# A one-core mLSTM layer with feed-forward: queries split behind the scores, token tiles transposed a turn later, the last output weights, the last chunk's output and the gate's start put in another order

## The chip, the cores and the metric

One core of a Trainium2 chip runs the whole kernel. The metric is the time of one execution in device microseconds. The kernel before was run three times and once more with the profiler.

## The reference

One layer over 2048 tokens of width 1024, in float32:

```python
xn = rmsnorm(h, norm_mix)
u = xn @ w_in                          # q, k (4 heads x 128), v, o (4 x 256), gates
h_fwd = mlstm_scan(q, k, v, g[0], g[1])
h_bwd = flip(mlstm_scan(flip(q), flip(k), flip(v), flip(g[2]), flip(g[3])))
h = rms(h_fwd + h_bwd, per head) * head_norm * sigmoid(o)
h1 = x + h @ w_out
h1 = h1 + square(relu(rmsnorm(h1) @ w1)) @ w2
gate = sigmoid(rmsnorm(h1) @ ple_gate_w + ple_gate_b)
out = rmsnorm(h1 + gate * (p @ ple_w))
...
def step(carry, xs):                   # mlstm_scan, one chunk of 128 tokens
    s = einsum('bhtd,bhsd->bhts', q_, k_) * d
    num = einsum('bhts,bhsv->bhtv', s, v_) + inter * einsum('bhtd,bhvd->bhtv', q_, C)
    den = sum(s) + inter * (q_ . n)
    h = num / max(abs(den), exp(-m_t))
    C = decay * C + einsum('bhsv,bhsd->bhvd', w * v_, k_)
```

## The kernel before, in words

Each float32 operand of a product is split into a high part (a copy rounded to fp32r on ScalarE, ACT) and a low part (a subtraction on VectorE, DVE, or GpSimd, POOL), and `mm3` (L185) makes a product of three matmuls from them. SyncE (SP) and POOL issue the loads and stores, in order on each queue. Instructions are written in a program order; the framework's scheduler then orders each engine's instructions by its own estimate of when they are ready, and each engine works through its list in that order. Most instructions have the line of a helper (L100), so they are told apart by the names of tiles.

Stages: the input projection; the backward scan, woven into the rest of the projection; then the forward scan over 16 chunks of 128 tokens, which also combines both directions and multiplies by `w_out`; the feed-forward part (up jobs, down jobs), written as seven products of half-size blocks each; and last, token tile by token tile, the gate, the second projection and the final norm.

**The forward scan (L683 to L821, L1372 to L1420).** In turn c the program works on several chunks at once. `ORDER` (L1373) is the list of steps of a turn; `step` (L1375) gives what each stands for:

- `n0`, `n1`: numerators of chunk c for both directions (`nums`): for each head a bank pn of six matmuls, then a copy nt on ACT. `s`: state update of chunk c (four banks pu, Cn on DVE, Chi on ACT), `sl` its low part Clo.
- `S`, `e`, `w`: scores pS of chunk c+1, the exponentials mb of its decay matrix (ACT, then a mask on POOL, L736), and their product (mb on DVE, pTh, pTl). `q`: `q_split`, the query operands, qsh on ACT and qsl on POOL (L748, L167). `k`: weighted keys wk. `v`: value operands vh, vl.
- `T`, `o0`, `o1`: of chunk c-1 the transposes pth, the gated hThi and hTlo, and the two halves of the output product pso with xt on DVE.
- `m`, `me`: norm of chunk c: rd, nt scaled on ACT and DVE, squares jk, then `rstd` (rsa, rsy, rst) and jk scaled by rsy.
- `d1`, `d2`, `d`, `p`: loads for chunks c+1 (vst, kt, cb) , c (og, xt) and c+2 (kq, mb, ib), and for c+2 ib times the queries on POOL (L726).

From turn `XC` = 7 on, three steps (`Tokens0.steps`, L1009) also prepare a finished token tile of the feed-forward part: `xl` loads it, `xn` normalises it (xs), `xt` transposes it (pt, zt) and stores it (x_d). All three stand in the same turn of `ORDER_X` (L1414); with them tile c-7 is made in turn c.

`TR` (L1390) mixes the end of the projection with chunk 0 and loads (`a0` to `a7`) and splits (`c0` to `c7`) the eight row blocks of `w_out`. `TAIL` (L1421) is the last chunk, with the first operands of the feed-forward part: `Z` loads, `U` block sums, `X` splits, `P` the first up job's left operands, `T15`, `y0`, `y1` the transposes and output of chunk 15.

Large tiles take one of 39 buffers of tag H (`Ht`), `raw`, `og`, `xt` and `zt` one of 7 of tag O (`Ot`). PSUM has four banks for pn, pu, pso and the product banks pa, pb, pg (`ps_mm`), three for transposes, pl and pc (`ps_tr`), one for scores and for the gate's token transposes (`ps_s`).

**The gate's start (L1468 to L1503).** The loads and splits of the gate weights `wgt` and of `wpl` (ple_w) and the first token tiles are hung into the last down jobs by `late`. Then, per token tile, `half` makes a half of the gate product pg from xTh, xTl and `wgt`, then pl from the embeddings and `wpl`, and the sum; `tr0` and `tr1` transpose the next tile in two halves, each into the single bank of `ps_s`.

Of the kernel before, what the change touches and what calls it, by code (L numbers as in the profile page):

```python
# [35 lines left out]
def hybrid_mlstm_kernel(  # L36
# [20 lines left out]
    x, p, out = x[0], p[0, 0], out[0]  # L57
# [7 lines left out]
    def ps_mm(name):  # L65
        return psm.tile([P, 512], F32, tag="mm", bufs=4, name=name)
# [614 lines left out]
    wo = [rows_w(w_out, k * P) for k in range(KD)]  # L681
# [500 lines left out]
    wgt = [rows_w(gate_w, k * P) for k in range(KD)]  # L1182
    wpl = [rows_w(ple_w, k * P) for k in range(2)]
# [32 lines left out]
    class Tok:  # L1216
# [21 lines left out]

        tr0, tr1 = (lambda self: self.tr(0)), (lambda self: self.tr(1))

        def half(self, n):

            if n == 0:
                self.ss = small("ssf")
            sl = slice(n * 512, (n + 1) * 512)
            pg = ps_mm("pg")
            tk = slice((self.t % 4) * P, (self.t % 4 + 1) * P)
            for k in range(KD):
                mm3(pg, self.hi[:, k], self.lo[:, k], wgt[k].hi[:, sl], wgt[k].lo[:, sl], k == 0, k == KD - 1)
# [39 lines left out]
    o, q = jobs[0, "o"], jobs[0, "q"]  # L1289
# [50 lines left out]
    for nm, pr in (("k", pa[0][0]), ("q", pa[0][1])):  # L1340
        e = pr.early()
# [7 lines left out]
    u1, u0 = jobs[0, "v"]  # L1349
# [20 lines left out]
    assert len(slots) == len(steps) - 8  # L1370

    ch = [Chunk(c) for c in range(NC)]  # L1372
    ORDER = "n0 d1 s e T S n1 d2 k w q sl m v d o0 o1 me p".split()  # L1373

    def step(c, nm):  # L1375

# [29 lines left out]
    def row_load(nm, src):  # L1406
        rowc[nm] = Ht(f"row_{nm}", [P, D])
        SP.dma_start(rowc[nm], src.partition_broadcast(P))


    XC = 7
    tp = {c: x0.steps(c - XC) for c in range(XC, XC + 8)}
    tp[XC][0] = lambda f=tp[XC][0]: (row_load("mlp", norm_mlp[0]), f())
    ORDER_X = "n0 d1 s e T S n1 d2 k w xl q sl m v d xn o0 o1 xt me p".split()  # L1414
    for c in range(1, NC - 1):
        for nm in ORDER_X if c in tp else ORDER:
            if nm in ("xl", "xn", "xt"):
                tp[c][("xl", "xn", "xt").index(nm)]()
            else:
                step(c, nm)()  # L1420
    TAIL = "d2 W n1 Z1 Z3 T n0 Z2 Z4 o0 m me P1 X1 T15 P2 o1 U3 U1 y0 X2 U2 X3 y1".split()  # L1421
    l = ch[NC - 1]
    u0 = up[0][0]
    extra = {"T15": l.transposes, "y0": lambda: l.out(0), "y1": lambda: l.out(1), "W": u0.left.dma,
             "P1": lambda: [f() for f in u0.prep[:3]], "P2": lambda: [f() for f in u0.prep[3:]],
             "X1": lambda: x0.split("B11"), "X2": lambda: x0.split("B21"), "X3": lambda: x0.split("T2")}
    extra |= {f"Z{i}": lambda nm=nm: x0.zload(nm) for i, nm in ((1, "B11"), (2, "B21"), (3, "B12"), (4, "B22"))}
    extra |= {f"U{i}": lambda i=i: x0.sums(f"T{i}") for i in (1, 2, 3)}
    for nm in TAIL:
        extra[nm]() if nm in extra else step(NC - 1, nm)()  # L1430
# [22 lines left out]
    n = ENTER[-1] + NQ  # L1453
# [14 lines left out]
    pp = [Early_p(t) for t in (0, 4, 8, 12)]  # L1468
    toks = [Tok(t, pp[t // 4]) for t in range(NC)]
    for g in range(4):  # L1470
# [55 lines left out]
```

## Time and profile before

| | us |
|---|---|
| three runs | 2489.95, 2493.55, 2499.76 (median 2493.55) |
| profiled execution | 2496.48 |
| its span, first to last instruction | 2494.8 |
| TensorE matmuls busy in it | 2415.3 |
| VectorE, ScalarE, GpSimd busy | 1525.7, 1134.5, 610.9 |
| TensorE granted clock, mean | 0.99 |

A stretch is read by four views: busy time by stretch (how long, how busy, at which granted clock), waits (who stood still for whom), the timeline of an engine (each instruction with the idle time before it and what ended it), and the durations of all instructions on a tile. `x4` counts instructions merged into a row. PE is TensorE; its matmuls overlap, so a row of 0.39 us can have its successor 0.23 us later.

### The profile page before, as it was taken

What the parts mean: (1) busy time and instruction counts of PE and PEld (TensorE: products, weight loads), DVE (VectorE), ACT (ScalarE), POOL (GpSimd) and SP (SyncE); (2) the same over time, 40 slices, a digit from 0 to 9 for tenths busy, and PEclk for the clock granted to TensorE, in tenths of its full rate; (3) what the DMA queues carried; (4) which work ended last, traced back from release to release, by engine and by line L of the source; (5) the groups of instructions that cost most, each with busy time, mean ns of one, the idle gap of its engine ahead of it and who ended that gap; (6) DMA issues with size and microseconds to landing.
All of it is one profiled execution on the core that took longest, in us unless ns stands there. A gap on an engine that the chain in (4) does not pass through costs nothing.

```text
span 2494.8 us, 31616 instructions
## 1 busy us (share of the span) xinstructions
PE 2415.3 (97%) x11413; PEld 1987.1 (80%) x11413; DVE 1525.7 (61%) x2533; ACT 1134.5 (45%) x2134; POOL 610.9 (24%) x609
## 2 busy tenths in 40 slices
PE   7999999998899999999999999999999999999998
PEld 6988898787778887788878888787887888777776
DVE  5152336456787888656775445766676667655665
ACT  5031324336667885443353333444443444445554
POOL 1040022124433334344733333111111111110000
PEclk9999999999999999999999999999999999999999
DMA  7177337867566765455763331467686776882211
GB/s 250 48 207 238 91 101 243 271 216 276 201 210 212 254 234 190 144 169 169 257 203 125 114 112 59 160 146 178 142 185 166 176 173 153 184 219 84 85 54 49
DMA packets 270134, 420.72 MB, mean 169 GB/s; under 512 B 46441, under 2 KB 181993, under 8 KB 269977
## 3 DMA queue, kind: packets, MB, share of 16 engines
q1 hardware_dynamic: 211416, 299.03, 36.7%
q0 software_dynamic: 58272, 119.15, 20.4%
q8 instruction: 89, 1.46, 0.2%
q14 instruction: 69, 0.56, 0.1%
q10 hardware_dynamic: 288, 0.52, 0.1%
HBM read 253.43 MB, written 165.01 MB: 168 GB/s over the span
## 4 chain that ended last, share of the span: by engine, by line
PE 52%; DVE 4%; DMA 3%; ACT 2%; issue 1%; SPq 0%; POOL 0%; ACTq 0%; DVEq 0%
PE pa L100 26%; PE pb L100 13%; PE pc L100 6%; PE pg L100 5%; DMA hst<-hid_d 1%; PE pl L100 1%; DMA wst<-in_mlp_w 1%; DVE op L100 1%; PE pt L100 1%; DVE h L100 1%; DMA z<-tz_d 1%; ACT L100 1%; DVE xs L100 1%; PE pso L100 1%; DVE rst L100 1%
## 5 line engine op out<-in xcount | busy, mean ns | idle before, releaser
L100 PE MATMUL pa<-op 128*128 128x512 f32 x3072 | 753.2, 394 | 7.6 <-ACT e L100 4.1
L100 PEld LDWEIGHTS pa<-op 128*128 128x128 f32 x3072 | 575.4, 188 | 147.6 <-ACT e L100 7.8
L100 PE MATMUL pb<-op 128*128 128x512 f32 x1536 | 384.3, 394 | 1.2 <-DVE op L100 0.8
L100 PEld LDWEIGHTS pb<-op 128*128 128x128 f32 x1536 | 288.1, 188 | 70.0 <-ACT e L100 1.2
L100 PE MATMUL psf<-xT,whi 128*128 128x512 f32 x1024 | 320.8, 394 | 0.0
L100 DVE TENSOR_TENSOR op<-sa,op 128x768 fp32r<-128x768 f32 (+2 forms) x160 | 167.6, 1053 | 137.9 <-ACT op L100 106.1
L1162 POOL DMA_DIRECT2D h_d<-o x96 | 93.1, 977 | 567.8 <-DVE o L100 507.3
L100 PEld LDWEIGHTS psf<-xT,whi 128*128 128x128 f32 x1024 | 191.3, 188 | 43.7
L100 ACT COPY e<-pa 128x512 f32<-128x512 f32 x160 | 93.7, 586 | 261.6 <-PE pa L100 260.9
L100 ACT CAST op<-sa 128x768 fp32r<-128x768 f32 (+2 forms) x160 | 139.6, 879 | 146.7 <-PE pb L100 66.6
L100 PE MATMUL psf<-xT,wlo 128*128 128x512 f32 x512 | 201.8, 394 | 0.0
L100 PE MATMUL pc<-op 128*128 128x512 f32 x768 | 191.6, 394 | 0.2 <-DVE op L100 0.2
L100 PEld LDWEIGHTS pc<-op 128*128 128x128 f32 x768 | 144.1, 188 | 34.1 <-DVE op L100 0.6
L100 PE MATMUL psv<-whi,xT 128*128 128x272 f32 (+2 forms) x720 | 160.9, 317 | 0.6 <-DVE xT L98 0.6
L100 PEld LDWEIGHTS psv<-whi,xT 128*128 128x128 f32 x720 | 118.6, 188 | 9.8 <-DVE xT L98 0.8
L100 DVE TENSOR_TENSOR op<-wst,op 128x512 fp32r<-128x512 f32 x96 | 108.6, 1134 | 28.7 <-ACT op L100 16.0
L884 POOL TENSOR_TENSOR sa<-wst 128x512 f32<-128x512 f32 x32 | 60.4, 1887 | 263.9 <-PE pb L100 167.6
L100 ACT CAST op<-wst 128x512 fp32r<-128x512 f32 x96 | 79.3, 834 | 93.8 <-DVE op L100 59.3
L100 DVE TENSOR_TENSOR wlo<-wst,whi 128x1024 fp32r<-128x1024 f32 (+2 forms) x64 | 77.1, 1214 | 60.4 <-ACT whi L100 49.4
L100 PE MATMUL psv<-wlo,xT 128*128 128x272 f32 (+2 forms) x360 | 114.0, 317 | 0.0
L100 PEld LDWEIGHTS psf<-xT,wlo 128*128 128x128 f32 x512 | 96.1, 188 | 22.4
L100 PE MATMUL pg<-whi,xTl 128*128 128x512 f32 x256 | 102.5, 400 | 0.0
(228 smaller groups left out, 4318.6 us busy)
## 6 DMA issues: line engine op xcount, KB each, us to landing
wst<-in_mlp_w SPq DMA_DIRECT2D x96, 512.0 KB
h_d<-o POOLq DMA_DIRECT2D x96, 512.0 KB, 12.8
hid_d<-e SPq DMA_DIRECT2D x128, 256.0 KB
hst<-hid_d SPq DMA_DIRECT2D x64, 384.0 KB
wst<-in_mlstm_w_in SPq DMA_DIRECT2D x44, 512.0 KB
vst<-v_d SPq DMA_DIRECT2D x31, 512.0 KB
raw<-in_x SPq DMA_DIRECT2D x16, 512.0 KB
kq<-kq_d SPq DMA_DIRECT2D x16, 512.0 KB
```

Of the source, the lines that this page charges most:

```text
L100: r = f(*a, **kw)
L884: eng.tensor_tensor(s[:, 0], r1[:, :, P:], r2[:, :, P:], op=add_)
L1162: G.dma_start(rows(h1_d, 2 * q + i), o[i], accum_op=add_)
```

## The change

- `q` moves in `ORDER` from behind `w` to right behind `S`, in `ORDER_X` too.
- `XC` is 6, so a tile is loaded and normalised in turns 6 to 13; its transposition `xt` is now made a turn later, behind `n1`, in turns 7 to 14.
- The splits `c6` and `c7` of the last two row blocks of `w_out` move from `TR` into turn 1, with a list of its own (`ORDER_1`, in which `q` keeps its old place).
- The output of chunk 15 (`y0`, `y1`) moves out of `TAIL` behind the first of the seven products of the first up job.
- At the gate's start the first tile's two gate products are made before the splits of ple_w and the first pl, and both transpositions of the second tile stand ahead of these; ple_w is loaded one down job later.

```diff
-        def half(self, n):
+        def gate(self, n):
+            sl = slice(n * 512, (n + 1) * 512)
+            self.pg = pg = ps_mm("pg")
+            for k in range(KD):
+                mm3(pg, self.hi[:, k], self.lo[:, k], wgt[k].hi[:, sl], wgt[k].lo[:, sl], k == 0, k == KD - 1)
+
+        def half(self, n, gate=True):
             if n == 0:
                 self.ss = small("ssf")
-            sl = slice(n * 512, (n + 1) * 512)
-            pg = ps_mm("pg")
+            if gate:
+                self.gate(n)
+            sl, pg = slice(n * 512, (n + 1) * 512), self.pg
             tk = slice((self.t % 4) * P, (self.t % 4 + 1) * P)
-            for k in range(KD):
-                mm3(pg, ...)
...
-    ORDER = "n0 d1 s e T S n1 d2 k w q sl m v d o0 o1 me p".split()
+    ORDER = "n0 d1 s e T S q n1 d2 k w sl m v d o0 o1 me p".split()
...
-        "n1 v b2 q m d c4 a6 me b3 c5 p c6 a7 c7").split()
+        "n1 v b2 q m d c4 a6 me b3 c5 p a7").split()
...
-    XC = 7
+    XC = 6
     tp = {c: x0.steps(c - XC) for c in range(XC, XC + 8)}
-    ORDER_X = "n0 d1 s e T S n1 d2 k w xl q sl m v d xn o0 o1 xt me p".split()
+    ORDER_1 = "n0 d1 s e T c6 S n1 d2 k w c7 q sl m v d o0 o1 me p".split()
+    ORDER_X = "n0 d1 s e T S q n1 xt d2 k xl w sl m v d xn o0 o1 me p".split()
     for c in range(1, NC - 1):
-        for nm in ORDER_X if c in tp else ORDER:
-            if nm in ("xl", "xn", "xt"):
-                tp[c][("xl", "xn", "xt").index(nm)]()
+        for nm in ORDER_X if c in tp or c - 1 in tp else ORDER if c > 1 else ORDER_1:
+            if nm == "xt":
+                tp.get(c - 1, [lambda: None] * 3)[2]()
+            elif nm in ("xl", "xn"):
+                tp.get(c, [lambda: None] * 3)[("xl", "xn").index(nm)]()
+            elif nm in ("c6", "c7"):
+                wo[int(nm[1])].prep()
             else:
                 step(c, nm)()
-    TAIL = "d2 W n1 Z1 Z3 T n0 Z2 Z4 o0 m me P1 X1 T15 P2 o1 U3 U1 y0 X2 U2 X3 y1".split()
+    TAIL = "d2 W n1 Z1 Z3 T n0 Z2 Z4 o0 m me P1 X1 o1 P2 T15 U3 U1 X2 U2 X3".split()
...
+    u0.post[0][:0] = [lambda: l.out(0), lambda: l.out(1)]
...
-            46: [wgt[6].prep, wgt[7].prep, wpl[0].dma, wpl[1].dma, toks[0].tr0, pp[0].split],
-            47: [wpl[0].prep, wpl[1].prep, toks[0].tr1, lambda: row_load("nf", norm_final)]}
+            46: [wgt[6].prep, wgt[7].prep, toks[0].tr0, pp[0].split],
+            47: [wpl[0].dma, wpl[1].dma, toks[0].tr1, lambda: row_load("nf", norm_final)]}
...
-        toks[t].half(0)
+        if t == 0:
+            toks[t].gate(0)
+            pg0 = toks[t].pg
+            nx.tr1()
+            toks[t].gate(1)
+            pg1 = toks[t].pg
+            wpl[0].prep()
+            wpl[1].prep()
+            toks[t].pg = pg0
+        toks[t].half(0, t > 0)
...
-        if nx:
+        if nx and t > 0:
             nx.tr1()
...
-        toks[t].half(1)
+        if t == 0:
+            toks[t].pg = pg1
+        toks[t].half(1, t > 0)
```

How the instructions stand on ACT in turn 1, from the second w_out cast (whi) in the turn on. Before:

```order
L100 CAST whi<-wst 128x1024
L100 ACTIVATE mb<-mb,gcol 128x128 x6
L100 CAST whi<-wst 128x1024
L100 ACTIVATE mb<-mb,gcol 128x128 x2
L100 CAST whi<-wst 128x1024
L100 COPY nt<-pn 128x257 x4
L100 CAST Chi<-Cn 128x1032
L100 CAST hThi<-og 128x512 x2
```

and with the change:

```order
L100 CAST whi<-wst 128x1024
L100 ACTIVATE mb<-mb,gcol 128x128 x3
L100 COPY nt<-pn 128x257 x4
L100 ACTIVATE mb<-mb,gcol 128x128 x5
L100 CAST Chi<-Cn 128x1032
L100 CAST hThi<-og 128x512 x2
L100 CAST whi<-wst 128x1024
L100 COPY nt<-pn 128x257 x4
L100 ACTIVATE wk<-kt,wcol 128x128 x4
L100 CAST pTh<-mb 128x512 x2
L100 CAST whi<-wst 128x1024
```

The four nt copies moved ahead of two of the casts, which now follow hThi and pTh.

ACT in turn 4, from the copy of the new state (Chi) to nt scaled by rd. Before:

```order
L100 CAST Chi<-Cn 128x1032
L100 CAST hThi<-og 128x512 x2
L100 COPY nt<-pn 128x257 x3
L100 ACTIVATE wk<-kt,wcol 128x128 x2
L100 COPY nt<-pn 128x257
L100 ACTIVATE wk<-kt,wcol 128x128 x2
L100 CAST pTh<-mb 128x512 x2
L100 CAST qsh<-ib 128x1024
L100 ACTIVATE nt<-nt,rd 128x256 x4
```

and with the change:

```order
L100 CAST hThi<-og 128x512 x2
L100 CAST qsh<-ib 128x1024
L100 COPY nt<-pn 128x257 x4
L100 ACTIVATE wk<-kt,wcol 128x128 x4
L100 CAST pTh<-mb 128x512 x2
L100 ACTIVATE nt<-nt,rd 128x256 x4
```

qsh moved from behind pTh to behind hThi, ahead of n1's nt copies.

ACT in a token turn, from the norm's rsy (four heads, 128x4) to Chi. Before:

```order
L100 ACTIVATE rsy<-rsa 128x4
L100 ACTIVATE rsy<-rsy 128x4
L100 ACTIVATE mb<-mb,gcol 128x128 x6
L100 COPY nt<-pn 128x257
L100 ACTIVATE mb<-mb,gcol 128x128 x2
L100 COPY zt<-pt 128x512 x2
L100 ACTIVATE jk<-nt,rsy 128x256 x4
L100 COPY nt<-pn 128x257 x3
L100 CAST Chi<-Cn 128x1032
```

and with the change:

```order
L100 ACTIVATE rsy<-rsa 128x4
L100 COPY nt<-pn 128x257
L100 ACTIVATE rsy<-rsy 128x4
L100 ACTIVATE mb<-mb,gcol 128x128 x2
L100 COPY nt<-pn 128x257
L100 ACTIVATE mb<-mb,gcol 128x128
L100 COPY nt<-pn 128x257
L100 ACTIVATE mb<-mb,gcol 128x128 x5
L100 ACTIVATE jk<-nt,rsy 128x256 x4
L100 CAST Chi<-Cn 128x1032
```

jk moved behind all four nt copies and all eight exponentials, and the token tile's copies zt left this place (they follow n1's copies).

## Rows read from the trace of the kernel before

**Rows 1.** Busy time by stretch: turns 1, 4, 7, 14 and the last chunk.
```profile
core 0: us, PE busy (x) PEld busy (x) DVE busy (x) ACT busy (x) POOL busy (x), PEclk, DMA share, GB/s
...
600.30:630.05 29.75, 22.38 (x126) 20.10 (x124) 21.11 (x34) 20.02 (x49) 11.68 (x12) 0.89 0.70 245
...
679.44:702.74 23.30, 21.52 (x126) 18.28 (x124) 17.70 (x35) 16.10 (x45) 8.65 (x11) 1.00 0.65 215
...
751.85:778.02 26.17, 23.78 (x125) 20.99 (x124) 18.95 (x36) 17.16 (x45) 8.43 (x10) 0.87 0.53 171
...
914.37:937.20 22.83, 21.46 (x133) 18.75 (x131) 18.89 (x44) 18.06 (x50) 7.68 (x8) 1.00 0.47 162
...
937.20:977.50 40.30, 35.32 (x169) 28.90 (x169) 32.58 (x44) 21.09 (x45) 12.88 (x6) 0.92 0.78 267
```

**Rows 2.** Waits of PE, 600 to 978 us: in total, times, longest.
```profile
PE pu L100 <- ACT nt L100: 16.1, 14, 7.4
PE pt L100 <- DVE xs L100: 10.3, 8, 1.4
```

**Rows 3.** Timeline of PE, single waits (start us, us, instruction, [idle before <-releaser]).
```profile
684.26 0.39 PE L100 MATMUL pu<-vh,wk 128*128 128x258 f32 x1 [1.28 <-ACT nt L100]
...
825.91 1.09 PE L100 MATMUL pt<-ident,xs 128*128 128x128 f32 x8 [1.35 <-DVE xs L100]
...
959.39 1.97 PE L100 MATMUL pth<-ident,jk 128*128 128x128 f32 x8 [3.33 <-ACT jk L100]
```

**Rows 4.** Timeline of ACT in turn 1.
```profile
611.10 1.04 ACT L100 CAST whi<-wst 128x1024 fp32r<-128x1024 f32 x1 [3.92 <-DMA wst<-in_mlstm_w_out]
612.05 1.19 ACT L100 COPY nt<-pn 128x257 f32<-128x257 f32 x4
```

**Rows 5.** Timeline of SP's queue in turn 1.
```profile
596.76 8.77 SPq L618 DMA_DIRECT2D kt<-kt_d  x5
605.63 0.38 SPq L202 DMA_DIRECT2D wst<-in_mlstm_w_out  x1
```

**Rows 6.** Timeline of ACT in turn 4.
```profile
681.37 1.71 ACT L100 ACTIVATE jk<-nt,rsy 128x256 f32<-128x256 f32 x4 [2.44 <-DVE rsy L100]
```

**Rows 7.** Timeline of DVE in turn 4.
```profile
696.29 3.82 DVE L100 SCALAR_TENSOR_TENSOR nt<-nt,rd 128x256 f32<-128x256 f32 x4
...
701.64 2.10 DVE L100 TENSOR_TENSOR vl<-vst,vh 128x1024 fp32r<-128x1024 f32 x1 [0.77 <-ACT vh L100]
```

**Rows 8.** Timeline of POOL in turn 4.
```profile
695.19 3.46 POOL L167 TENSOR_TENSOR qsl<-ib,qsh 128x1024 fp32r<-128x1024 f32 x1 [8.25 <-ACT qsh L100]
...
701.36 3.53 POOL L726 TENSOR_TENSOR ib<-kq,ib 128x512 f32<-128x512 f32 x2 [2.51 <-DMA ib<-in_d]
```

**Rows 9.** Timeline of DVE in the last chunk, where no query subtraction runs.
```profile
946.68 1.69 DVE L100 SCALAR_TENSOR_TENSOR nt<-nt,rd 128x256 f32<-128x256 f32 x4 [0.64 <-ACT nt L100]
```

**Rows 10.** Instructions on tile nt: duration ns min/median/max, first and last start.
```profile
L100 DVE SCALAR_TENSOR_TENSOR nt<-nt,rd x52: 469/474/2641, 647.0 to 932.5; 128x256 f32<-128x256 f32 x52
```

**Rows 11.** Instructions on tile mb, same columns.
```profile
L100 DVE TENSOR_TENSOR mb<-pS,mb x26: 679/684/693, 640.5 to 924.0; 128x512 f32<-128x512 f32 x26
```

**Rows 12.** Timeline of ACT in a token turn.
```profile
823.87 1.85 ACT L100 ACTIVATE mb<-mb,gcol 128x128 f32<-128x128 f32 x6
```

**Rows 13.** Timeline of DVE in the same token turn.
```profile
826.37 1.25 DVE L100 TENSOR_TENSOR rsy<-rsy,rst 128x4 f32<-128x4 f32 x1
```

**Rows 14.** Timeline of PE at the gate's start.
```profile
2235.22 0.40 PE L100 MATMUL pg<-whi,xTh 128*128 128x512 f32 x1
2235.45 0.40 PE L100 MATMUL pg<-wlo,xTh 128*128 128x512 f32 x1
...
2242.30 1.11 PE L100 MATMUL pt<-ident,xs 128*128 128x128 f32 x4 [5.76 <-DVE xTl L100]
```

**Rows 15.** Busy time by stretch behind that wait, columns as in rows 1.
```profile
2242.30:2250.00 7.70, 7.70 (x30) 6.31 (x31) 3.17 (x5) 4.83 (x7) 2.13 (x2) 0.80 0.88 279
```

**Rows 16.** Timeline of ACT at the gate's start.
```profile
2239.34 1.04 ACT L100 CAST whi<-wst 128x1024 fp32r<-128x1024 f32 x1 [6.96 <-DMA wst<-in_ple_w]
...
2243.41 1.04 ACT L100 CAST whi<-wst 128x1024 fp32r<-128x1024 f32 x1 [2.54 <-DMA wst<-in_ple_w]
```

More of the change, by code (lines that the diff above doesn't have):

```diff
@@ L1239, in hybrid_mlstm_kernel @@
         tr0, tr1 = (lambda self: self.tr(0)), (lambda self: self.tr(1))
-        def half(self, n):
+        def gate(self, n):
[4 more added lines that the diff above has]
+        def half(self, n, gate=True):
             if n == 0:
                 self.ss = small("ssf")
-            sl = slice(n * 512, (n + 1) * 512)
-            pg = ps_mm("pg")
+            if gate:
+                self.gate(n)
+            sl, pg = slice(n * 512, (n + 1) * 512), self.pg
             tk = slice((self.t % 4) * P, (self.t % 4 + 1) * P)
-            for k in range(KD):
-                mm3(pg, self.hi[:, k], self.lo[:, k], wgt[k].hi[:, sl], wgt[k].lo[:, sl], k == 0, k == KD - 1)
             pl = ps_tr("pl")
@@ L1408, in row_load @@
         SP.dma_start(rowc[nm], src.partition_broadcast(P))
-    XC = 7
+    XC = 6
     tp = {c: x0.steps(c - XC) for c in range(XC, XC + 8)}
     tp[XC][0] = lambda f=tp[XC][0]: (row_load("mlp", norm_mlp[0]), f())
-    ORDER_X = "n0 d1 s e T S n1 d2 k w xl q sl m v d xn o0 o1 xt me p".split()
+    ORDER_1 = "n0 d1 s e T c6 S n1 d2 k w c7 q sl m v d o0 o1 me p".split()
+    ORDER_X = "n0 d1 s e T S q n1 xt d2 k xl w sl m v d xn o0 o1 me p".split()
     for c in range(1, NC - 1):
-        for nm in ORDER_X if c in tp else ORDER:
-            if nm in ("xl", "xn", "xt"):
-                tp[c][("xl", "xn", "xt").index(nm)]()
+        for nm in ORDER_X if c in tp or c - 1 in tp else ORDER if c > 1 else ORDER_1:
[5 more added lines that the diff above has]
+                wo[int(nm[1])].prep()
             else:
                 step(c, nm)()
-    TAIL = "d2 W n1 Z1 Z3 T n0 Z2 Z4 o0 m me P1 X1 T15 P2 o1 U3 U1 y0 X2 U2 X3 y1".split()
+    TAIL = "d2 W n1 Z1 Z3 T n0 Z2 Z4 o0 m me P1 X1 o1 P2 T15 U3 U1 X2 U2 X3".split()
     l = ch[NC - 1]
     u0 = up[0][0]
-    extra = {"T15": l.transposes, "y0": lambda: l.out(0), "y1": lambda: l.out(1), "W": u0.left.dma,
+    extra = {"T15": l.transposes, "W": u0.left.dma,
              "P1": lambda: [f() for f in u0.prep[:3]], "P2": lambda: [f() for f in u0.prep[3:]],
```

## The prediction

> **What bounds the kernel now.** The page's table of engines has TensorE (PE) busy nearly all the time, so time can only come out of stretches in which PE stands still or runs at its lower clock. To find them I read the busy time by stretch, cut at the first matmul of each chunk turn (n0, the numerators of one direction) [rows 1]. It shows three kinds of turn. Turn 1 takes 29.75 us. Turns 2 to 6, without token work, run from 630.05 to 751.85: 121.80 us, 24.4 each. Turns 8 to 14, which also transpose one token tile each, run from 778.02 to 937.20: 159.18 us, 22.74 each. The turns that do more are shorter. In them PE is busy 21.5 us at granted clock 1.00; turns 1 and 7 have 0.89 and 0.87, so they ran in part at the lower of the two levels (1.2 instead of 2.4 GHz). Then the waits of PE over these turns [rows 2], and each in its place [rows 3]: without token work it is pu (the state update) waiting for ScalarE's (ACT) nt copies to free a PSUM bank, with short waits for vl and xt beside it; in the token turns it is pt waiting for xs, 10.3 us in eight times; behind the last chunk's scores it is pth waiting for jk.
>
> So the chunk loop is a cycle through ACT and VectorE (DVE): jk, nt copies, state, scores, rd, nt scaled, squares, vh and vl, the next rsy, jk. PE waits where this cycle is late.
>
> **Turn 1.** PE's longest wait, 7.4 us [rows 2], comes because the nt copies stand on ACT behind the cast of the last w_out tile, whose transfer came late [rows 4]: SyncE (SP) issued it at 605.63, behind five key loads that took 8.77 us [rows 5]. The change puts the two last w_out casts behind hThi and behind pTh, with the nt copies ahead of both; on SP the last w_out load now stands ahead of the five key loads. The cast is then needed only by the last eighth of the first output product, some 14 us into the turn, about when ACT reaches it. A turn without stalls is a token turn's busy 21.46 less its eight pt (1.09) [rows 3], 20.4 us. I take 21.5: **-8.2 us** (ends: -9.4 at 20.4; -4 if half the wait comes back as the output product waiting for the cast).
>
> **Turns 2 to 6.** What makes jk late? In the turn that starts at 679.44 ACT begins jk 1.93 us in, after waiting for rsy [rows 6], then does three exponentials, and only then the first nt copy; pu waits 1.28 us for it [rows 3]. rsy is late because the squares are, and these wait for nt scaled on DVE: four instructions took 3.82 us, the first held until POOL's query subtraction qsl ended at 698.65 [rows 7, 8]. Where no such subtraction runs, the same four take 1.69 [rows 9]; over all turns one lasts 474 ns in the median and 2641 at most [rows 10]. The change issues qsh and qsl right behind the scores, and in the order qsh stands ahead of n1's nt copies on ACT, so qsl is done when nt is scaled. That brings squares, vh, vl and rsy forward by 3.82 - 1.69 = 2.1 us: jk starts 0.2 us before the turn instead of 1.9 behind. With one exponential ahead of it where there were three, the first nt copy ends some 2.3 us in (1.71 for jk, 0.3 for each of the others) [rows 4, 6], before PE has finished n0's 24 pn, which it did at 684.26 - 1.28, 3.5 us in. pu's wait goes, vl's with it, and with the stalls the lower clock. What is left is 20.4 us of PE work. I take 21.5, because POOL's two key-by-weight products ib still meet DVE somewhere: in this turn they held vl to 2.10 [rows 7, 8]. 121.8 becomes 107.5: **-14.3 us** (ends: 20.6 a turn, -18.8; 23.0 a turn, -6.8).
>
> Which DVE instructions can qsl hold in its new place? mb from pS reads PSUM and lasted 679 to 693 ns in all 26 [rows 11]; og and the state update read PSUM too. Those left are hTlo, rd, wk and pTl, due some microseconds later. The Trainium skill (SBUF — State Buffer, "Who interferes with whom") says that VectorE and GpSimd share one port pair under an exclusive lock, and that a VectorE instruction with two SBUF inputs is blocked for the whole of a GpSimd instruction that reads SBUF. By this rule moving qsl frees nothing in sum, it only picks another victim. The rows agree that the wait lasts to qsl's end. By the chain above the new victims have slack; if they have none, it is the second rival below.
>
> **Turn 7** took 26.17 us and becomes the first with a token transposition at the new place: as below, 22.4, **-3.8 us**.
>
> **Turns 8 to 14.** pt's wait (1.35) [rows 3] goes for certain: the tile is normalised a turn ahead. But this wait also covered jk. In the new order ACT does eight exponentials (0.3 each: six took 1.85) [rows 12] and four nt copies ahead of jk, the first of them when the first six pn end, 0.8 us into the turn: with rsy's 0.5, jk begins at about 0.8 + 2.4 + 1.4 + 0.5 = 5.1, and PE reaches pth, now strewn among n1's pn, at about 5.4, when the first jk is just done. Small waits between them make 21.7 a turn of 21.46. POOL's order now has both ib ahead of the masks; if they land on the short rst chain each holds it by about 1.1 (one did before: 1.25 for a 128x4 instruction) [rows 13], and jk with it: up to some 23.9. I take 22.4: 159.2 becomes 156.8, **-2.4 us** (ends: 21.4, -9.4; 23.9, +8.1).
>
> **The last chunk** (937.20 to 977.50, through the first feed-forward product, rows 1). Token tile and pt's wait leave it, about 1.9. The first product, twelve matmuls or 2.9 us, now stands between the output of chunk 14 and pth, where PE waited 3.33 [rows 3]. Clock 0.92 over 40.3 us means 6.4 us at the lower level, 3.2 lost. All of it would be 8.0. But that product's operands are made by DVE and POOL in turn, and the rst chain of the last jk stands among them. I take **-4.8 us** (ends -8, -2).
>
> **The gate's start.** PE waits 5.76 us for xTl [rows 14] and then has clock 0.80 for 7.7 us, 1.5 lost [rows 15]. The wait is an order on ACT: the next tile's xTh stood behind a cast of ple_w, which waited 6.96 us for its transfer [rows 16]. Now both transpositions of the next tile and both halves of the gate product (48 matmuls, 0.23 us apart, 11 us) [rows 14] stand ahead of the casts. The second cast ended at 2244.45, and its low part is ready about a microsecond later; PE now needs it at about 2246.7. I take **-5.5 us** (ends -7.3; -1 if the loads, issued one step later, land 5 us later).
>
> Nothing else is priced: PE has the same matmuls, loads and stores of the output are the same, and the first 600 us keep their order.
>
> **The sum.** -8.2 - 14.3 - 3.8 - 2.4 - 4.8 - 5.5 = -39.0 us against the profiled execution's 2496.5: 2457.5. That execution is 2.9 us above the median of the runs shown (2493.55), so I forecast **2455 us**.
>
> **Rivals.** First, the token turns gain nothing. For it: ib held DVE in both turns that I read. Against it: ib must land within some 2 us. At 23.9 instead of 22.4 in eight turns it costs 12: 2467 us.
> Second, qsl's hold moves with it: hTlo or rd is late by the same 2.1 us and the cycle keeps its length. Turns 2 to 6 stay at 24.4 (+14.3), the token turns at 22.7 (+2.4): 2472 us. Against it: rd waits for n1's last copy anyway.
> Third, slower: the earlier split and an xs kept into the next turn hold three more of the 39 large SBUF buffers (tag H) in the middle of a turn. If kq, mb or ib of the chunk after next waits for one of them, the whole of SP's queue waits behind it, and mb and qsh come late in every turn. POOL already waited 2.51 us for ib's transfer [rows 8]. Against it: ib's reader qsh comes some 8 us later, so only what a load slips beyond that counts. It decides from 39/13 = 3 us a turn on; at 4.5 us over 13 turns the kernel is 20 us slower than now, 2513.
> Fourth, the last w_out tile still comes late: turn 1 keeps 4 us more, 2459, inside my range.
>
> **How the numbers follow.** Forecast (the fourth rival with it) 0.64, first rival 0.2, second 0.12, third 0.04. The favourable ends all together give -57 us, the others -10; neither is likely whole. The range is 2441 to 2477, about -52 to -16, and takes in both mild rivals. A change under 0.5% (12.5 us) can't be told from none here. Faster than that are the forecast, the first rival and nearly all of the second, 0.9; slower the third, 0.04; within 0.5% the rest, 0.06.
>
> **What would show it.** Right: of the nt scaled on DVE none above 1 us; no pu wait above 0.5 in turns 2 to 6 and clock 1.00 there; no pt wait; turn 1 near 21.5; pg without the 5.76. Wrong: pth waiting for jk over 1 us in the token turns (first rival); hTlo or rd above 1.5 us with turns near 24 (second); ACT or POOL waiting for kq, mb or ib, issued late (third).

## The result and the profile after

The changed kernel takes **2464.32 us** in the median of four runs (2461.31 to 2469.05) against 2493.72 before, a ratio of **0.9882** with the interval 0.9856 to 0.9908. Timed once more later, in another set of runs (e11), it took 2469.65 against 2495.76: 0.9896 (0.9882 to 0.9911). The forecast was 2455, the range 2441 to 2477, "faster" 0.9. The time is in the range and the sign is right; the gain is 29 us where 39 were forecast.

The profiled execution took 2461.31 us, 35.2 less than the one before. Cut at the same places (a turn begins at the first n0 matmul; the last chunk ends where the second feed-forward product begins; the gate's stretch runs from the last twelve-matmul pa ahead of it to the second pl of the second token tile):

| stretch | before | forecast | changed | difference, forecast / measured |
|---|---|---|---|---|
| turn 1 | 29.75 | 21.5 | 23.09 | -8.2 / -6.7 |
| turns 2 to 6 | 121.80 | 107.5 | 107.11 | -14.3 / -14.7 |
| turn 7 | 26.17 | 22.4 | 22.42 | -3.8 / -3.8 |
| turns 8 to 14 | 159.18 | 156.8 | **167.12** | -2.4 / **+7.9** |
| last chunk | 40.30 | 35.5 | 32.79 | -4.8 / -7.5 |
| gate's start | 48.20 | 42.7 | 40.48 | -5.5 / -7.7 |
| ahead of turn 1 | 600.30 | 600.3 | 597.75 | 0 / -2.6 |

The last row is not the change's: the order there is the same, and later profiles begin turn 1 anywhere from 597.6 to 602.4. These 2.6 us are part of the 35.2 between the two profiles; the medians differ by 29.

Busy time by stretch of the changed kernel, columns as in [rows 1]: turns 1, 2, 4 and 12, then turns 2 to 6, turns 8 to 14, the last chunk and the gate's start.

```profile
597.75:620.84 23.09, 20.88 (x126) 18.18 (x124) 20.40 (x33) 19.52 (x47) 10.75 (x12) 1.00 0.86 318
620.84:645.12 24.28, 21.49 (x125) 18.24 (x124) 18.74 (x40) 16.75 (x48) 8.20 (x11) 1.00 0.67 211
665.60:686.62 21.02, 20.94 (x125) 18.19 (x124) 15.43 (x34) 15.96 (x47) 7.53 (x11) 1.00 0.78 258
846.72:870.78 24.06, 21.55 (x133) 19.00 (x132) 20.49 (x40) 18.24 (x51) 8.56 (x10) 1.00 0.67 233
620.84:727.95 107.11, 104.13 (x622) 90.75 (x620) 81.41 (x177) 82.53 (x232) 37.47 (x50) 1.00 0.67 225
750.37:917.49 167.12, 153.14 (x926) 134.39 (x924) 140.37 (x281) 128.20 (x357) 55.27 (x68) 0.99 0.71 237
917.49:950.28 32.79, 31.67 (x161) 26.42 (x160) 29.15 (x41) 20.32 (x42) 8.03 (x5) 1.00 0.79 266
2195.28:2235.76 40.48, 40.02 (x183) 32.03 (x182) 22.75 (x37) 23.05 (x38) 4.27 (x4) 1.00 0.74 182
```

Turn 4, 23.3 us in [rows 1], is now nearly all PE work (20.94 of 21.02). The clock, 0.89 in turn 1 and 0.92 in the last chunk before, is 1.00 in both. The token turns are the opposite: PE's own work there stayed near 21.5 a turn, and the turns grew.

Waits of PE of the changed kernel, 597 to 978 us, as in [rows 2]:

```profile
PE pth L100 <- ACT jk L100: 6.6, 8, 1.6
PE pn L100 <- DVE Cn L100: 5.3, 4, 1.8
PE pu L100 <- ACT nt L100: 3.6, 7, 1.1
PE pso L100 <- ACT nt L100: 1.9, 2, 1.4
```

pu's 16.1 us are 3.6, pt's 10.3 are gone. In their place stand two waits that the loop of chunks 8 to 14 did not have: pth for jk, and the first pn of n1 for Cn. Both come from one place on DVE. Turn 12, which starts at 846.72, timelines of DVE, POOL, ACT and PE:

```profile
848.38 2.27 DVE L100 TENSOR_TENSOR rst<-rsa,rsy 128x1 f32<-128x1 f32 x1 [0.63 <-ACT rsy L100]
...
851.69 1.29 DVE L100 SCALAR_TENSOR_TENSOR xs<-raw,rsy,row_mlp 128x1024 f32<-128x1024 f32 x1
...
854.27 0.15 DVE L100 TENSOR_TENSOR rsy<-rsy,rst 128x4 f32<-128x4 f32 x1
...
847.53 0.55 POOL L706 DMA_DIRECT2D Clo<-cb_d  x1
848.09 2.54 POOL L726 TENSOR_TENSOR ib<-kq,ib 128x512 f32<-128x512 f32 x2
...
854.45 1.71 ACT L100 ACTIVATE jk<-nt,rsy 128x256 f32<-128x256 f32 x4 [2.73 <-DVE rsy L100]
...
853.93 0.39 PE L100 MATMUL pn<-vh,pTh 128*128 128x258 f32 x1 [1.82 <-DVE Cn L100]
855.01 0.44 PE L100 MATMUL pth<-ident,jk 128*128 128x128 f32 x2 [0.69 <-ACT jk L100]
```

POOL's two ib products run from 848.09 to 850.63. The first rst of the token's norm, one number per partition, begins 0.3 us after them and ends 0.02 us after them: 2.27 us for an instruction that takes 0.16 when nothing holds it. The token's chain, xs (1.29), the heads' chain and Cn stand behind it in DVE's list. jk begins 7.7 us into the turn; the prediction's chain had 5.1. That is the prediction's first rival, at its price of 23.9 us a turn (167.12 / 7); the run, 2464, lies nearer the rival's 2467 than the forecast's 2455.

### The profile page after: what moved, and what is told of

Read it like the earlier page. It is cut to its first block, busy times and chain, and to the rows that moved or that the text cites. A ratio compares the mean times of both kernels' runs of the same rounds, so it can differ in the third digit from the quotient of the medians.

```text
span 2459.6 us, 31654 instructions
## 1 busy us (share of the span) xinstructions
PE 2401.7 (98%) x11413; PEld 1977.9 (80%) x11413; DVE 1517.4 (62%) x2533; ACT 1132.5 (46%) x2134; POOL 592.2 (24%) x609
## 4 chain that ended last, share of the span: by engine, by line
PE 52%; DVE 4%; ACT 2%; DMA 2%; issue 1%; SPq 0%; POOL 0%; ACTq 0%; DVEq 0%; POOLq 0%
PE pa L100 27%; PE pb L100 13%; PE pc L100 7%; PE pg L100 4%; PE pl L100 1%; DVE h L100 1%; ACT L100 1%; DMA hst<-hid_d 1%; DVE xs L100 1%; PE pt L100 1%; DMA wst<-in_ple_w 1%; DMA wst<-in_mlp_w 1%; DVE op L100 1%; DVE rst L100 1%; ACT g L100 0%
## 5 line engine op out<-in xcount | busy, mean ns | idle before, releaser
L100 ACT CAST op<-sa 128x768 fp32r<-128x768 f32 (+2 forms) x160 | 139.6, 879 | 148.1 <-PE pb L100 69.0
L100 PEld LDWEIGHTS psf<-xT,wlo 128*128 128x128 f32 x512 | 96.1, 188 | 22.4
L100 PE MATMUL pso<-whi,hThi 128*128 128x512 f32 x256 | 102.1, 400 | 3.2 <-ACT nt L100 1.9
```

What stands on the lines that cost most here:

```text
L100: r = f(*a, **kw)
```

## The experiments

All twelve kernels are built from the two. The table gives the same stretches of each profile, in us; the ratio is to the kernel before, timed in the same set.

| | turn 1 | 2 to 6 | 7 | 8 to 14 | last chunk | median | ratio, interval |
|---|---|---|---|---|---|---|---|
| e4 only q | 30.3 | 105.4 | 20.9 | 152.7 | 40.4 | 2471.44 | 0.9906 (0.9877 to 0.9934) |
| e6 turn 1, output, gate | 23.1 | 123.5 | 24.9 | 159.1 | 37.0 | 2478.04 | 0.9918 (0.9889 to 0.9947) |
| e5 change, no shift | 24.4 | 110.1 | 20.5 | 153.0 | 38.8 | 2455.27 | 0.9827 (0.9798 to 0.9855) |
| e3 q late in token turns | 23.1 | 106.6 | 25.4 | 161.6 | 32.7 | 2459.07 | 0.9856 (0.9828 to 0.9885) |
| e1 ib behind masks | 23.1 | 109.0 | 22.4 | 154.6 | 32.8 | 2452.03 | 0.9828 (0.9799 to 0.9856) |
| e9 ib on VectorE | 24.4 | 106.7 | 21.2 | 154.5 | 33.8 | 2453.44 | 0.9833 (0.9813 to 0.9853) |
| e2 e1, xn late | 23.1 | 109.0 | 21.5 | 148.1 | 32.6 | 2447.82 | 0.9811 (0.9783 to 0.9840) |
| e7 e2, q in turn 1 | 24.5 | 107.9 | 21.5 | 148.2 | 32.8 | 2448.78 | 0.9801 (0.9770 to 0.9832) |
| e8 e7, ib from turn 3 | 25.6 | 105.3 | 21.5 | 148.2 | 32.9 | 2447.16 | 0.9794 (0.9766 to 0.9823) |
| e10 | 22.1 | 112.0 | 21.5 | 148.2 | 32.7 | 2447.02 | 0.9806 (0.9788 to 0.9824) |
| e12 | 22.1 | 108.2 | 21.5 | 148.2 | 33.8 | 2446.71 | 0.9806 (0.9793 to 0.9819) |
| e11 change again | 24.4 | 109.4 | 22.4 | 171.5 | 32.7 | 2469.65 | 0.9896 (0.9882 to 0.9911) |

**e1: ib behind the masks.** The same work on POOL, tied to another place from turn 8 on:

```diff
+    PRE = 9
...
-                G.affine_select(out=self.mb[:, d], ...)
+                last = G.affine_select(out=self.mb[:, d], ...)
+            if self.c >= PRE:
+                for d in range(2):
+                    with tc.issue_after(last.ins):
+                        last = G.tensor_tensor(self.ib[:, d], self.kq[:, 1], self.ib[:, d], op=ALU.mult)
...
-            f |= {"d": n2.dma, "p": n2.pre}
+            f |= {"d": n2.dma} | ({"p": n2.pre} if c + 2 < PRE else {})
```

> The changed kernel, with POOL's two ib products tied behind the two masks in turns 8 to 14 (same work, other place). Theory A (in the changed kernel ib stands ahead of the masks and holds the short rst instructions of the norm, so jk starts 7.5 us into the turn): jk starts about 5 us into the turn, no rst above 0.6 us, turns 8 to 14 take 152 to 157 us where the changed kernel took 167.1, the profiled run 2446 to 2452. Rival B (jk is late because VectorE carries too much, and because ACT has the first nt copy ahead of rsy): jk still starts near 7 us, the seven turns stay at 165 to 168, the run at 2459 to 2465. Rival C (ib is then late for qsh, and the hold goes to hTlo): qsh waits, the seven turns take 165 or more.

Measured: 154.64 for turns 8 to 14, 12.5 us less than the changed kernel; 2452.03. The turn that starts at 841.24, DVE, POOL and ACT:

```profile
842.90 0.16 DVE L100 TENSOR_TENSOR rst<-rsa,rsy 128x1 f32<-128x1 f32 x1 [0.64 <-ACT rsy L100]
...
845.34 0.44 DVE L100 TENSOR_SCALAR rst<-rst 128x4 f32<-128x4 f32 x1
...
846.88 2.54 POOL L743 TENSOR_TENSOR ib<-kq,ib 128x512 f32<-128x512 f32 x2
...
846.27 1.71 ACT L100 ACTIVATE jk<-nt,rsy 128x256 f32<-128x256 f32 x4
```

ib starts when the chain is done, the rst that took 2.27 takes 0.16, and jk begins 5.03 us into the turn, where the prediction's chain without a hold (5.1) had put it. Theory A holds; B and C fall.

**e9: ib on VectorE**, to tell POOL's hold from the place in the list:

```diff
-                G.tensor_tensor(self.ib[:, d], self.kq[:, 1], self.ib[:, d], op=ALU.mult)
+                (V if self.c > XC else G).tensor_tensor(self.ib[:, d], self.kq[:, 1], self.ib[:, d], op=ALU.mult)
```

> The changed kernel with both ib products of turns 6 to 13 computed by VectorE instead of POOL; the program order is the change's. If it is POOL's work that holds the rst instructions (and not their place in VectorE's list): no rst or rsy above 0.6 us in turns 8 to 14 although VectorE now carries two products of 0.5 to 0.7 us more a turn, jk starts 5 to 6 us into the turn, and the seven turns take 153 to 160 us where the changed kernel took 167.1. If VectorE's own load bounds the chain, the two products cost what the hold cost: 165 or more.

Measured: 154.46 us for turns 8 to 14. DVE of the turn that starts at 815.06:

```profile
816.72 0.16 DVE L100 TENSOR_TENSOR rst<-rsa,rsy 128x1 f32<-128x1 f32 x1 [0.64 <-ACT rsy L100]
...
818.77 0.69 DVE L100 TENSOR_TENSOR ib<-kq,ib 128x512 f32<-128x512 f32 x1
819.37 0.60 DVE L100 TENSOR_SCALAR rst<-rst 128x4 f32<-128x4 f32 x1
```

Both products now stand in the middle of DVE's own chain and cost 0.69 each, and the seven turns are still 12.7 us shorter. What cost the time was POOL working beside DVE, not the amount of work on DVE. The expectation's 5 to 6 us for jk was just missed in turns 10 to 14 (6.05), where the products stand ahead of the end of the chain.

**e4: only q**, on the kernel before:

```diff
-    ORDER = "n0 d1 s e T S n1 d2 k w q sl m v d o0 o1 me p".split()
+    ORDER = "n0 d1 s e T S q n1 d2 k w sl m v d o0 o1 me p".split()
...
-    ORDER_X = "n0 d1 s e T S n1 d2 k w xl q sl m v d xn o0 o1 xt me p".split()
+    ORDER_X = "n0 d1 s e T S q n1 d2 k w xl sl m v d xn o0 o1 xt me p".split()
```

> The kernel before with q moved right behind the scores in both orders, and nothing else. If q alone makes the gain of turns 2 to 6: they take 106 to 110 us instead of 121.8, with nt scaled never above 1 us and no pu wait above 0.5; if the freed ACT order or turn 1 does it, they stay above 115. In the token turns ib stands behind the first mask as before: theory A expects 159 or less for turns 8 to 14 (pt still waits for xs), rival D 165 or more. Turn 1 and the last chunk as before, within 2 us. The run: 2496 less 13 to 17, about 2482.

Measured: 105.38 for turns 2 to 6, no nt scaled above 0.49 us; the first reading holds, q alone does it. In the token turns q alone gains too: 152.67, and turn 7 20.88. The run was therefore too cautiously expected: 2471, not 2482. Busy time of its turns 8 to 14, and PE's wait for the token tile over 600 to 940 us:

```profile
755.43:908.10 152.67, 150.58 (x925) 132.34 (x923) 130.35 (x282) 128.46 (x353) 53.61 (x68) 1.00 0.75 255
...
PE pt L100 <- DVE xs L100: 2.4, 7, 0.6
```

pt's eight waits, 10.3 us [rows 2], are now 2.4 us in sum although no tile moved: xs begins 0.3 to 0.8 us into turns 8 to 14 instead of 1.1 to 1.5, now that nt scaled isn't held.

**e6: turn 1, the last chunk's output and the gate alone**, with the changed kernel's `ORDER_1`, `TAIL` and gate, but `q` at its old place in all turns and a tile's three steps in one turn; the edit is shown against the changed kernel:

```diff
-    ORDER = "n0 d1 s e T S q n1 d2 k w sl m v d o0 o1 me p".split()
+    ORDER = "n0 d1 s e T S n1 d2 k w q sl m v d o0 o1 me p".split()
...
-    XC = 6
+    XC = 7
...
-    ORDER_X = "n0 d1 s e T S q n1 xt d2 k xl w sl m v d xn o0 o1 me p".split()
+    ORDER_X = "n0 d1 s e T S n1 d2 k w xl q sl m v d xn o0 o1 xt me p".split()
...
```

> The kernel before with only the w_out splits in turn 1, the last chunk's output behind the first product and the gate's start as changed; q and the token tiles as before. If these three act alone as in the changed kernel: turn 1 takes 23.1 us (6.7 less), the last chunk 32.8 (7.5 less), the gate's start 7.7 less, turns 2 to 14 as before within 3 us, the run 22 less than before, about 2474. If the last chunk's gain needs the token tile out of it: the last chunk takes 35 or more and the run is near 2477.

Measured: turn 1 as in the changed kernel, 23.10. The last chunk took 37.0, the second reading: moved output alone gains 3.3 there, and pth still waits 3.34 for jk. The gate's start took 40.3, 7.9 less than before, so that part acts alone as expected; all that lies behind the last chunk is 6.2 us shorter than before (8.0 in the changed kernel). The run: 2478.04, 20 less than before.

**e5: the change without the shift of the token tiles:**

```diff
-    XC = 6
+    XC = 7
...
-    ORDER_X = "n0 d1 s e T S q n1 xt d2 k xl w sl m v d xn o0 o1 me p".split()
+    ORDER_X = "n0 d1 s e T S q n1 d2 k w xl sl m v d xn o0 o1 xt me p".split()
...
```

> The changed kernel without the shift of the token tiles (XC 7, xl, xn and xt of a tile in one turn again), all else as changed, the early q too. Theory A' (q alone brings the token turns to 21.9, the shift makes the scheduler put both ib ahead of the masks, onto the rst chain, and that is the loss): turns 8 to 14 take 150 to 155 us where the changed kernel took 167.1, turn 7 21 to 22, pt waits for xs by about 0.4 a turn, the run is at 2443 to 2449. Rival (the loss comes from q's or the tail's new place together with the tokens): 163 or more, the run above 2456.

Measured: 153.04 for turns 8 to 14 and 20.5 for turn 7, as expected of theory A'. The run, 2455.27, lies between the two expectations, because the shift also does good: without it the last chunk takes 38.8 instead of 32.8 (pth waits 4.1 us for jk; what holds jk there stands in the account of the last chunk below). So the shift costs 14 us in turns 8 to 14 and gives 6 back in the last chunk; by the medians (2464.32 and 2469.65 against 2455.27, from three sets) the change is 9 to 14 us slower than it would be without it.

**e3: q at its old place in the token turns only.**

```diff
-    ORDER_X = "n0 d1 s e T S q n1 xt d2 k xl w sl m v d xn o0 o1 me p".split()
+    ORDER_X = "n0 d1 s e T S n1 xt d2 k xl w q sl m v d xn o0 o1 me p".split()
```

> The changed kernel with q back behind xl in the token turns only (qsh and qsl late there, as before), all else as changed. Theory A (ib's new place does the harm): ib still stands ahead of the masks, and qsl holds nt scaled again by 2.1 us, so turns 8 to 14 take 167 or more. Rival D (the early query split does the harm in the token turns, through hTlo held to 2.47 us): turns 8 to 14 fall back to 156 to 160, the run to about 2452.

Measured: 161.6, between the two, and turn 7 went up to 25.4: 187.0 for turns 7 to 14 together, 2.5 less than the changed kernel. Neither reading holds. With q late the heads' rst chain stands ahead of xs, and jk begins 2.5 to 6.1 us into the turn although ib still holds single rst instructions to 1.3 us; in exchange nt scaled takes 3.8 again. The run suggests that the order of the two norms on DVE matters beside ib's place; e2 tests that.

**e2: as e1, the token's norm behind the chunk's.**

```diff
-    ORDER_X = "n0 d1 s e T S q n1 xt d2 k xl w sl m v d xn o0 o1 me p".split()
+    ORDER_X = "n0 d1 s e T S q n1 xt d2 k xl w sl m v d o0 o1 me xn p".split()
```

> As e1, and the token tile's norm (xn) issued behind the chunk's norm (me), so that xs (1.29 us on VectorE) and its own rst chain no longer stand between the four heads' rst instructions. Theory A with xs as a second part: jk starts another 1.3 us or more earlier than in e1, turns 8 to 14 take 150 to 153 us (21.5 a turn is TensorE's own work). If xs costs nothing once ib is away: the same as e1 within 1 us. If the norm's order was all of it and ib nothing, e1 stays at 167 and this one falls alone.

Measured: 148.12, 6.5 less than e1 and below the expected 150. Busy time of turns 8 to 14 and of turn 9:

```profile
754.51:902.63 148.12, 147.54 (x925) 132.10 (x924) 127.58 (x275) 127.44 (x353) 51.82 (x68) 1.00 0.81 269
775.47:796.69 21.22, 21.22 (x133) 18.90 (x132) 18.12 (x39) 18.41 (x52) 7.49 (x10) 1.00 0.85 287
```

PE doesn't wait at all in turn 9. Four later kernels with these two edits took 148.2 in the same turns; the change itself took 167.1 and 171.5 (e11).

**e7: as e2, with q right behind the scores in turn 1 too.**

```diff
-    ORDER_1 = "n0 d1 s e T c6 S n1 d2 k w c7 q sl m v d o0 o1 me p".split()
+    ORDER_1 = "n0 d1 s e T c6 S q n1 d2 k w c7 sl m v d o0 o1 me p".split()
```

> As e2, and q right behind the scores in turn 1 as well. If turn 2's 24.0 us come from turn 1's late query subtraction (nt scaled and vl held at 618 to 622 us): turn 2 falls to 20.5 to 21, turn 1 stays at 22.5 to 23.5, the run at 2443 to 2445. If turn 2 is late because of the w_out splits in turn 1 themselves: turn 2 stays above 23, the run at 2446 to 2449.

Measured: turn 2 fell to 22.39, between the readings, and turn 1 rose to 24.51: 46.9 together, 47.1 in e2. Nothing is won: with the query split early, PE's output product in turn 1 waits 2.34 us for the nt copies, where it waited 1.36.

**e8: as e7, ib tied behind the masks from turn 3 on.**

```diff
-    PRE = 9
+    PRE = 4
```

> As e7, and both ib products tied behind the masks from turn 3 on, not only in the token turns. If turn 4's 23.1 us in e1 and e2 (21.0 in the changed kernel) is the same hold, ib that starts 0.8 us earlier and lands on the rst chain of the chunk's norm: turn 4 falls to 20.5 to 21, all of turns 2 to 6 within 20.4 to 21.1, the run 2 us below e7. If it has another cause, turn 4 stays at 23.

Measured: turn 4 21.3 instead of 23.95 (e7), which speaks for the first reading though not quite 20.5 to 21; turns 3 to 6 84.0 instead of 85.5; the runs differ by less than their spread. Why turn 4 took 21.02 in the changed kernel and 23.14 in e1, with the same order there, two pieces show. DVE and POOL at the end of turn 3, the changed kernel first:

```profile
664.51 0.16 DVE L100 TENSOR_TENSOR rst<-rst,rsy 128x4 f32<-128x4 f32 x1
664.71 0.17 DVE L100 TENSOR_SCALAR rst<-rst 128x4 f32<-128x4 f32 x1
664.91 0.16 DVE L100 TENSOR_TENSOR rsy<-rsy,rst 128x4 f32<-128x4 f32 x1
...
665.09 2.57 POOL L726 TENSOR_TENSOR ib<-kq,ib 128x512 f32<-128x512 f32 x2 [8.79 <-DMA ib<-in_d]
```

and e1:

```profile
664.11 0.16 DVE L100 TENSOR_TENSOR rst<-rst,rsy 128x4 f32<-128x4 f32 x1
664.30 1.28 DVE L100 TENSOR_SCALAR rst<-rst 128x4 f32<-128x4 f32 x1
665.62 1.23 DVE L100 TENSOR_TENSOR rsy<-rsy,rst 128x4 f32<-128x4 f32 x1
...
664.26 2.57 POOL L728 TENSOR_TENSOR ib<-kq,ib 128x512 f32<-128x512 f32 x2 [8.37 <-DMA ib<-in_d]
```

ib waits for its transfer. Where that lands 0.02 us behind the end of rsy, the chain is free; where it lands 0.4 us earlier relative to the chain, two instructions are held and the turn is 2.1 us longer.

**e10: the best pieces together:** e2's, `PRE = 4`, and in turn 1 the cast `c6` behind `n1`.

```diff
-    ORDER_1 = "n0 d1 s e T c6 S n1 d2 k w c7 q sl m v d o0 o1 me p".split()
+    ORDER_1 = "n0 d1 s e T S n1 c6 d2 k w c7 q sl m v d o0 o1 me p".split()
```

> As e2 (ib behind the masks, the token's norm behind the chunk's), ib behind the masks from turn 3 on as in e8, q in turn 1 as changed, and in turn 1 the split of the last but one w_out block issued behind n1 instead of ahead of the scores. TensorE's output product waited 1.36 us in turn 1 because the nt copies stood behind that cast: turn 1 falls from 23.1 to about 22, turn 2 stays at 24, turns 3 to 6 at 84, 7 to 14 at 169.6; the median 2444 to 2447, 0.7% below the changed kernel. If the cast is then late for the product instead: turn 1 stays at 23 or more and pso waits for wlo.

Measured: turn 1 22.12 as expected, but turn 2 27.97: turn 1 won 1.0 us, turn 2 lost 4.0. DVE and PE at its start:

```profile
620.44 3.95 DVE L100 TENSOR_TENSOR vl<-vst,vh 128x1024 fp32r<-128x1024 f32 x1
...
624.45 0.58 PE L100 MATMUL pn<-vl,pTh 128*128 128x258 f32 x1 [4.30 <-DVE vl L100]
```

**e12: as e10, ib tied from turn 2 on.**

```diff
-    PRE = 4
+    PRE = 3
```

> As e10, with ib tied behind the masks from turn 2 on instead of turn 3. In e10 turn 2 took 27.97 us: vl lasted 3.95 us beside qsl and ib on POOL, and pn waited 4.3 us for it. If that ib was the cause: vl ends by 622, the wait of pn for vl falls below 2 us, turn 2 takes 23 to 25.5, turn 1 22.1 as in e10, the median 2442 to 2445. If qsl alone holds vl: turn 2 stays at 27 or more and the median at 2446 to 2448.

Measured: pn waits 1.55 us for vl, which took 1.21, and turn 2 is 24.37: ib was the cause of e10's. The median, 2446.71, missed the 2442 to 2445. In its profile the part ahead of turn 1, the same in both, took 4.7 us more than in e10's. From the start of turn 1 to the end of the span e12 took 1843.5 us, e2 1844.8, the changed kernel 1861.9, the kernel before 1894.5. So e12 beats both kernels, by about 1.9% (0.9793 to 0.9819) against before; against e2 it is not told apart.

**e11: the changed kernel again**, without an edit.

> The changed kernel once more, beside e10 on the same chip: 2461 to 2466, turns 8 to 14 at 166 to 168; if the order of ib against rst is settled by a microsecond of DMA, single turns differ from the first profile by about 1 to 2 us.

Measured: 2469.65 and 171.45 for turns 8 to 14, both above what was expected. Single turns differ from the first profile by up to 2 us (turn 8: 25.97 and 23.93). In the three longest (25.97, 25.60, 24.75) the granted clock was 0.93; what PE waits for there is the same, jk and Cn.

## Why the prediction was right, and where it was wrong

**What bounds the kernel** was read rightly: the cycle through ACT and DVE, not PE. That the sum came within 10 us is in part luck: turns 8 to 14 lost 10.3 us against the forecast and turn 1 lost 1.6, and 4.9 came back from the last chunk and the gate's start, which gave more than forecast.

**Turns 2 to 6, right, and for the reason given.** e4 shows that q alone does it. nt scaled was at most 2641 ns [rows 10] and is now:

```profile
L100 DVE SCALAR_TENSOR_TENSOR nt<-nt,rd x60: 474/480/491, 614.7 to 927.9; 128x256 f32<-128x256 f32 x60
...
L100 DVE TENSOR_TENSOR hTlo<-og,hThi x32: 679/684/2471, 607.9 to 940.8; 128x512 fp32r<-128x512 f32 x32
...
L167 POOL TENSOR_TENSOR qsl<-ib,qsh x14: 2382/2401/2534, 615.0 to 905.4; 128x1024 fp32r<-128x1024 f32 x14
```

The hold did move, as the second rival said: hTlo now lasts up to 2471 ns, and an rd up to 2364. But they have slack: in e2, with hTlo up to 1785 and rd up to 2350, PE is busy for 147.5 of 148.1 us. The rival's mechanism is there, its price is not. Within the stretch the shares were off: turns 3 to 6 take 20.4 to 21.0, less than the 21.5 taken, and turn 2 takes 24.3, where q is still late in turn 1 (20.5 in e4 and 22.4 in e7, where it is early).

**Turns 8 to 14, wrong: the step that failed is "I take 22.4", the size given to ib on the rst chain.** The text had the order (both ib ahead of the masks), the victim, and the price (23.9 a turn, +8.1); it gave that 0.2 and weighed a "must land within some 2 us" against it. The sign that it named for this rival came: pth waits for jk, up to 1.6 us. In turns 10 to 13 ib did not land by chance. On POOL it stood behind the loads Chi and Clo, which wait for PE's output product; on DVE the norm stands behind xt, which waits for the same product. So in turns 11 to 13 ib began 1.4 us into the turn and the first rst 1.7, and in turn 10 the victim was the instruction ahead of them, an rsa that took 3.06. In turns 8, 9 and 14 ib had another place or landed later (0.8, 1.0 and 2.8 us into the turn) and met the chain too, for some 1.2 us at a time. The other step there, that pt's wait "goes for certain" with the shift, was right, but e4 shows that q alone leaves 2.4 of the 10.3 us: the shift was paid for something that was nearly had already.

**Turn 1, right, off by 1.6.** PE's output product waited 1.36 us for nt copies that stood behind the moved cast, a price that the sum didn't have:

```profile
609.61 0.50 PE L100 MATMUL pso<-whi,hThi 128*128 128x512 f32 x1 [1.36 <-ACT nt L100]
...
608.25 1.04 ACT L100 CAST whi<-wst 128x1024 fp32r<-128x1024 f32 x1
609.20 1.19 ACT L100 COPY nt<-pn 128x257 f32<-128x257 f32 x4
```

e10 moved the cast and got 1.0 of it back in that turn. 23.1 was also the better of two outcomes: with the same order e5, e9 and e11 took 24.4, because pn waited 1.50 us for Cn and not 0.20. DVE and POOL in the changed kernel, and below them in e11:

```profile
599.26 1.23 DVE L100 TENSOR_TENSOR wlo<-wst,whi 128x1024 fp32r<-128x1024 f32 x1 [0.62 <-ACT whi L100]
599.72 4.15 POOL L726 TENSOR_TENSOR ib<-kq,ib 128x512 f32<-128x512 f32 x2
...
599.20 5.20 DVE L100 TENSOR_TENSOR wlo<-wst,whi 128x1024 fp32r<-128x1024 f32 x2 [0.62 <-ACT whi L100]
599.66 2.52 POOL L726 TENSOR_TENSOR ib<-kq,ib 128x512 f32<-128x512 f32 x2
```

In the first, wlo holds ib; in the second, ib holds wlo, and DVE comes to Cn 1.2 us later. **Turn 7** came as forecast.

**The last chunk, right, larger: -7.5 of a possible 8.0.** e6 and e5 tell the parts apart: the moved output alone gives 3.3, and the rest comes only with the shift of the token tiles, which takes pth's wait for jk away. POOL and DVE show how, before and then with the change:

```profile
954.18 2.33 POOL L889 TENSOR_TENSOR sa<-wst 128x512 f32<-128x512 f32 x1
955.29 1.24 DVE L100 TENSOR_SCALAR rst<-rst 128x4 f32<-128x4 f32 x1
...
924.55 1.29 POOL L890 TENSOR_TENSOR sa<-wst,sa 128x512 f32<-128x512 f32 x1
933.44 0.15 DVE L100 TENSOR_TENSOR rst<-rst,rsy 128x4 f32<-128x4 f32 x1
```

It is the hold of turns 8 to 14 once more. Before, POOL's four block sums sa for the first product run 13.4 to 21.6 us into the chunk, among the rst chain of the last jk, and three of its instructions take 1.2 us. With the shift the loads of that product's weights are issued 12 us earlier against the chunk's start, the sums run 2.0 to 8.4 us into the chunk, and the chain, 14.7 to 18, is free. All four profiles without the shift (before, e4, e5, e6) have the late sums and a wait of 3.2 to 4.1; none of the ten with it has either. So the discount for "operands made by DVE and POOL in turn" named the right place, and the shift moved the sums out of it, which the sum had not foreseen; why the loads come earlier was not tested.

**The gate's start, right, larger: -7.7, beyond its end of -7.3.** The casts of ple_w wait for their transfers as before,

```profile
2213.41 1.05 ACT L100 CAST whi<-wst 128x1024 fp32r<-128x1024 f32 x1 [5.98 <-DMA wst<-in_ple_w]
```

but PE has 48 matmuls to do meanwhile. The same stretch before, columns as in [rows 1]:

```profile
2222.83:2271.03 48.20, 41.94 (x183) 33.33 (x183) 23.07 (x38) 22.94 (x38) 4.27 (x4) 0.93 0.64 161
```

The wait of 5.76 went, and one of 0.44 ahead of it; a new one of 0.46 came. PE's busy time fell by 1.9 (41.94 to 40.02) with the clock at 1.00, where 1.5 was forecast.

**The third and fourth rivals** did not come: no load of kq, mb or ib was late enough to count, and the last w_out cast was in time.

## What to carry to other kernels

When two engines hold each other off, moving one of the two pieces of work is only half an edit: list where the other piece will then run, and what releases it. If the same event releases it and a chain of short instructions on the critical cycle, they meet in every turn; tie it behind an instruction that only comes when the chain is over (here the masks), rather than leave its place to the scheduler's estimate. And take the edits of a change apart before stacking them: here the early query split alone gave 24 us, the three other places together 20, and the shift of the token tiles, good for the last chunk, took some 9 to 14 back in all.

## What the runs showed of the hardware that was not expected

- The hold does not depend on the size of the instruction that is held. An rst on 128x1, 0.16 us when free, took 2.27 beside two ib products of 1.27 each, and was not let in between them; an rsa on 128x4 took 3.06 in turn 10. Elsewhere two instructions in a row were held by one product each (1.28 and 1.23 in e1 above).
- It goes both ways. qsl took 3134 to 3457 ns (median 3220) in the kernel before and 2382 to 2534 at its new place. Before, it met two DVE instructions in turn: Clo, which ran or began when qsl began and held it (in turn 4 both start at 695.19 and Clo takes 1.18), and then nt scaled, which qsl held. The Trainium skill (SBUF — State Buffer, "Who interferes with whom") says that whoever issues first gets the shared ports, and that the other one blocks; the trace agrees there: some 0.8 us on POOL, then 2.1 on DVE.
- By the profile's starts, the first is not always the one that is let through, so that rule can't be applied to the starts alone. In turn 1, shown above, wlo begins 0.46 us ahead of ib in both kernels; in one it runs through in 1.23, in the other it is held to the end of both ib products. The rsa of 3.06 also began 0.5 us ahead of ib. In all three cases POOL was issuing a DMA when the DVE instruction began; what decides was not tested.
- Instructions with one SBUF input are held as well: the `TENSOR_SCALAR` rst on 128x4 took 1.28 us in e1. The same section of the Trainium skill names `tensor_scalar` among the operations that can take both port pairs when their operands allow it, and the trace agrees in so far as this one was held.
- A transfer that lands 0.4 us earlier against a chain can make a turn 2.1 us longer, with the same order of instructions there (the changed kernel and e1, turn 4). Turns that alternate in length without a change of work, as turns 2 to 6 did before, may come from this too; that was not tested.
